# The gated product of two feed-forward blocks, kept in PSUM and split into its halves from there

## The chip, the cores and the metric

The kernel runs on one core of a Trainium2 chip. The metric is the device time of one execution in microseconds (us): a median of several runs of each kernel. The engines are named as the profile names them: PE (TensorE, matmuls), PEld (its weight loads), DVE (VectorE), ACT (ScalarE), POOL (GpSimd) and SP (SyncE, which issues DMAs). SBUF is the working memory of the core; PSUM is the memory into which PE writes, in eight banks.

## The reference

Two layers run over 512 latent tokens and 256 context tokens of width 1024. Layer 0 mixes the tokens with gated DeltaNet and retention heads, layer 1 with differential softmax attention; each layer ends in a gated feed-forward block with 2816 hidden features:

```python
def conv_ffn(h, rows, w_gate, w_up, w_conv, w_down):
    a = h @ w_gate
    a = dwconv2d_centred(a.reshape(bt, rows, lt // rows, D_FF), w_conv).reshape(bt, lt, D_FF)
    return (jax.nn.silu(a) * (h @ w_up)) @ w_down
```

A residual add and a layer norm follow. All inputs are float32. The context tokens pass through the block of layer 0 only, since layer 1 returns latent tokens alone.

## The kernel before

Every large matrix product is made of three: each operand is split into a high half (a copy rounded to fp32r) and a low half (the operand less its high half), and PE sums high by high, high by low and low by high in one PSUM bank. For activations and weights alike the high half is thus a copy on ACT and the low half a subtraction on DVE or POOL. The helper `split` (lines 139 to 148) does this; most weight splits put their low half (`wlo`) on POOL, and their operations all carry lines 147 and 148.

`ffn` (line 1396) is called twice: for layer 0 with 768 tokens (`has_ctx`, "the first block" below, about 690 to 1260 us of the span) and for layer 1 with 512 tokens ("the second block", from about 1685 us to the end). The 2816 hidden features are 22 groups of 128, called f, taken two at a time in 11 steps, called p. For every f, `gate_up` (line 1441) does the following.

- PE makes the gate sum `pg` (tile g_ps) and the up sum `pu` (u_ps) for the 512 latent tokens, each in one bank, and in the first block both for the context in one bank `pc` (c_ps: columns 0 to 255 gate, 256 to 511 up). Each of these tiles has two buffers, so f+2 takes the bank of f.
- ACT (line 1465) writes the middle tap of the 3x3 convolution into the SBUF tile `ac`, and DVE adds the eight others (line 1476), reading g_ps. The context has a convolution of three taps (lines 1480 to 1486).
- ACT takes silu of `ac` in place (line 1487).
- DVE multiplies the up sum by it, back into `ac` (lines 1488, 1490).
- `split` makes the high half `hh` on ACT (line 147) and the low half `hl` on DVE (line 148) from `ac`.

Then (`down`, line 1413, called at line 1522) PE multiplies hh and hl of the step before with a slice of the down weights into d_ps: a group of 6 matmuls for each of the 128-token tiles and each half of the width, 12 groups for a step of the first block and 8 in the second. d_ps has two banks in the first block and four in the second. In the first block DVE takes each group out with a multiplication by the gate (tile gt, line 1425), and line 1523 adds gt to `acc` in SBUF, in turn on POOL and on DVE. In the second block the gate is already in the down weights and DVE adds d_ps straight to `acc` (line 1523). Between steps 0 and 1 DVE multiplies all `acc` tiles by a row of the norm (line 1505: `acc`, `lng` and the result lie in SBUF). After step 10 the last two down products follow, and the layer norm.

Instructions of an engine run in one order. That order is chosen when the program is built, by a planner that goes by priorities (mostly the order of the code) and by its own estimate of when operands will be ready; semaphores are added where an operand or a buffer comes from another engine. So a changed instruction may also take another place among those of its engine.

Of the kernel before, what the change touches and what calls it, by code (L numbers as in the profile page):

```python
# [11 lines left out]
F32 = mybir.dt.float32  # L12
# [11 lines left out]
LAT, CTX = 512, 256  # L24
# [73 lines left out]
class Net:  # L98
# [1297 lines left out]
    def ffn(self, l, has_ctx, acc, dst, key):  # L1396
# [4 lines left out]
        v, g, s_ = nc.vector, nc.gpsimd, nc.scalar  # L1401
# [5 lines left out]
        with ExitStack() as st0:  # L1407
# [5 lines left out]
            def down(w, x, t, n, ps, first=True, last=True, gated=False):  # L1413

                (wh, wl), (xh, xl) = w, x
                steps = [(wi, xi, k) for k in range(2) for xi, wi in ((xh, wh), (xh, wl), (xl, wh))]
                for j, (wi, xi, k) in enumerate(steps):
                    self.mm(ps, xi[:, k, t * P:(t + 1) * P], wi[:, k, n * 512:(n + 1) * 512],
                            start=(first and j == 0), stop=(last and j == len(steps) - 1))
                if not last:  # L1420
                    return
                if gated:
                    return acc[t][:, n * 512:(n + 1) * 512], ps
                gt = gtp.tile([P, 512], F32, tag="gt", name="gt")
                v.tensor_mul(gt, ps, gates[0 if t < NLT else 1][:, n * 512:(n + 1) * 512])  # L1425
                return acc[t][:, n * 512:(n + 1) * 512], gt

            with ExitStack() as st:
                wf = None if key else self.pool(st0, f"wffn{l}", bufs=2)
                fp = self.pool(st, f"ffn{l}", bufs=2)  # L1430
                wf = wf or self.pool(st, f"wffn{l}")
                if key:

                    self.wps = [self.wp]
                else:
                    self.wps = [self.wp, self.wp, wf, wf]
                self.wcount = 0
                gp = self.pool(st, f"ps_g{l}", bufs=2, space=PSUM)
                upp = self.pool(st, f"ps_u{l}", bufs=2, space=PSUM)
                cpp = self.pool(st, f"ps_c{l}", bufs=2, space=PSUM) if has_ctx else None  # L1440
                def gate_up(p):
                    cols = slice(p * 256, (p + 1) * 256)
                    uw = [self.unit([w[:, cols]]) for w in (wg, wu)]
                    hh = hidp.tile([P, 2, NTK], F32R, tag="hh", name="hh")
                    hl = hidp.tile([P, 2, NTK], F32R, tag="hl", name="hl")
                    for i in range(2):
                        f = 2 * p + i
                        cw = [fc[:, t * NFF + f:t * NFF + f + 1] for t in range(9)]
                        pg = gp.tile([P, 512], F32, tag="g", name="g_ps")
                        pu = upp.tile([P, 512], F32, tag="u", name="u_ps")  # L1450
                        pc = cpp.tile([P, 512], F32, tag="c", name="c_ps") if has_ctx else None
                        for j, (w, pl) in enumerate(zip(uw, (pg, pu))):
                            d = [(pl, 0, LAT)]
                            if p == 0:
                                d = [(pl[:, :256], 0, 256), (pl[:, 256:], 256, 256)]
                            if has_ctx:
                                c = (pc[:, j * CTX:(j + 1) * CTX], LAT, CTX)
                                d = [c] + d if p == 0 else d + [c]
                            if p == 0:
                                for one in d:  # L1460
                                    self.proj_fm(w, i * P, [one])
                            else:
                                self.proj_fm(w, i * P, d)
                        ac = fp.tile([P, NTK], F32, tag="ac", name="ac")
                        s_.activation(ac[:, :LAT], pg, AF.Copy, scale=cw[4])  # L1465
                        R, C = LAT // GRID_W, GRID_W
                        av = ac[:, :LAT].rearrange("p (r c) -> p r c", r=R)
                        pv = pg.rearrange("p (r c) -> p r c", r=R)
                        for di in (-1, 0, 1):
                            for dj in (-1, 0, 1):  # L1470
                                if di == 0 and dj == 0:
                                    continue
                                r0, r1 = max(0, -di), R - max(0, di)
                                c0, c1 = max(0, -dj), C - max(0, dj)
                                o = av[:, r0:r1, c0:c1]
                                v.scalar_tensor_tensor(out=o, in0=pv[:, r0 + di:r1 + di, c0 + dj:c1 + dj],  # L1476
                                                       scalar=cw[(di + 1) * 3 + dj + 1], in1=o,
                                                       op0=ALU.mult, op1=ALU.add)
                        if has_ctx:
                            s_.activation(ac[:, LAT:], pc[:, :CTX], AF.Copy, scale=cw[4])  # L1480
                            o = ac[:, LAT + 1:TOK]
                            v.scalar_tensor_tensor(out=o, in0=pc[:, 0:CTX - 1], scalar=cw[3], in1=o,
                                                   op0=ALU.mult, op1=ALU.add)
                            o = ac[:, LAT:TOK - 1]
                            v.scalar_tensor_tensor(out=o, in0=pc[:, 1:CTX], scalar=cw[5], in1=o,
                                                   op0=ALU.mult, op1=ALU.add)
                        s_.activation(ac, ac, AF.Silu)  # L1487
                        v.tensor_mul(ac[:, :LAT], pu, ac[:, :LAT])  # L1488
                        if has_ctx:
                            v.tensor_mul(ac[:, LAT:], pc[:, CTX:], ac[:, LAT:])  # L1490
                        self.split(ac, hh[:, i, :], hl[:, i, :], v)
                    hid[p] = (hh, hl)

                self.lo_engs, self.lo_count = "v" if l else "vgvv", 0
                gate_up(0)
                if key:
                    self.wps = [wf, self.wp, self.wp, self.nextw]
                    self.wcount = 0
                lnb = self.row(self.pool(st, f"flnb{l}"), a["ln_b"][l, 0], "lnb")
                rst = ExitStack()  # L1500
                lng = self.row(self.pool(rst, f"flng{l}"), a["ln_g"][l, 0], "lng")
                for r in (lng, lnb):
                    self.pin(s_.activation(r, r, AF.Copy, scale=ALPHA))
                for t in tiles:
                    self.pin(v.tensor_mul(acc[t], acc[t], lng))  # L1505
                gate_up(1)
                self.lo_engs = "g"
                self.cparts = 1
                gates = self.gate_rows(lnp, l, 1, 2 if has_ctx else 1)
                last = None if key else self.affine_rows(lnp, l, 1)  # L1510
                rst.close()
                gtp = self.pool(st, f"fgt{l}", bufs=GTB)
                for p in range(1, NP):
                    if p > 1:
                        gate_up(p)
                    if p < NP - 1:
                        w = self.unit_rows(wd[(p - 1) * 256:p * 256, :], None if key else gates[0])
                        x = hid.pop(p - 1)
                        for t in tiles:
                            for n in range(2):  # L1520
                                ps = dp.tile([P, 512], F32, tag="d", name="d_ps")
                                o, gt = down(w, x, t, n, ps, gated=not key)
                                (v if n or not key else g).tensor_add(o, o, gt)
                    if 2 <= p < 2 + len(tiles):
                        t = tiles[p - 2]
                        self.pin(g.tensor_add(acc[t], acc[t], lnb))
                if key:
                    self.wps = [self.wp]
                ws = [self.unit_rows(wd[p * 256:(p + 1) * 256, :], None if key else gates[0]) for p in (NP - 2, NP - 1)]
# [5 lines left out]
            with ExitStack() as st:  # L1535
# [6 lines left out]
                for gi, grp in enumerate(groups):  # L1542
# [6 lines left out]
                    for t in grp:  # L1549
                        st_ = self.ln_stats()  # L1550
                        for n in range(2):
                            if gi == 0:
                                ps = pss[t, n]
                            else:
                                ps = next(dps).tile([P, 512], F32, tag="d", name="d_ps")
# [290 lines left out]
```

## Time and profile before

| what | value |
|---|---|
| median of 3 runs | 2064.56 us (2062.54 to 2068.04) |
| profiled execution, own time | 2061.71 us |
| its span, first to last instruction | 2059.9 us |
| mean granted PE clock | 0.98 of full |
| busy: PE, PEld, DVE, ACT, POOL | 94%, 81%, 60%, 35%, 38% |

The profile is of one execution, taken by the hardware profiler; durations below are from it. "Busy" counts the time in which an engine executes. A timeline row gives the start and the length of one instruction, or of several merged ones (x2), and in brackets how long the engine had been idle before it, and which instruction ended that wait. In the lists by line, three durations stand for the shortest, the median and the longest.

### The profile page before, as it was taken

How to read it: one execution, taken by the hardware profiler on the slowest of the kernel's cores; microseconds unless marked ns; L12 is line 12 of the kernel's file. 1: busy time of each engine (PE TensorE's matmuls, PEld its weight loads, DVE VectorE, ACT ScalarE, POOL GpSimd, SP SyncE). 2: the span in 40 equal slices, each digit the busy share in tenths (PEclk: the TensorE clock that was granted, in tenths of full speed). 3: DMA queues.
4: the chain of work that ended last, by engine and by line, in shares of the span. 5: the costliest groups of instructions: out<-in, count | busy, mean ns of one | idle time of the engine just before them, and what ended most of it. 6: DMA issues, size and time to landing. Idle time of an engine off the chain costs nothing. (4 is left out here: it accounts for less than half of the span.)

```text
span 2059.9 us, 33511 instructions
## 1 busy us (share of the span) xinstructions
PE 1940.8 (94%) x13766; PEld 1669.9 (81%) x13766; DVE 1229.4 (60%) x2430; ACT 721.5 (35%) x1273; POOL 776.3 (38%) x416
## 2 busy tenths in 40 slices
PE   7999999999898999999999998999997989999997
PEld 5877677788898988888888887989886987888886
DVE  3344645443467686666666656456667687756667
ACT  4432343433334522222222225454555343323221
POOL 1233223212322254554544434122213126756572
PEclk9999999999999999999999999999998999999999
DMA  9456334465624221111111112011103143323221
GB/s 290 129 169 181 111 116 141 133 179 175 184 74 132 93 82 62 62 62 62 62 62 62 62 62 90 21 42 42 42 32 103 52 144 102 99 85 102 82 82 41
DMA packets 198113, 201.33 MB, mean 98 GB/s; under 512 B 21336, under 2 KB 186808, under 8 KB 197960
## 3 DMA queue, kind: packets, MB, share of 16 engines
q1 hardware_dynamic: 195832, 196.78, 30.4%
q10 hardware_dynamic: 2128, 2.41, 0.4%
q8 instruction: 108, 1.77, 0.4%
q14 instruction: 45, 0.37, 0.1%
HBM read 185.89 MB, written 13.27 MB: 97 GB/s over the span
## 5 line engine op out<-in xcount | busy, mean ns | idle before, releaser
L148 POOL TENSOR_TENSOR wlo<-raw,whi 128x512 fp32r<-128x512 f32 (+2 forms) x158 | 416.5, 2657 | 498.4 <-ACT whi L147 457.3
L1476 DVE SCALAR_TENSOR_TENSOR ac<-g_ps,fconvT,ac 128x441 f32<-128x441 f32 (+2 forms) x352 | 243.9, 694 | 190.9 <-ACT ac L1465 181.2
L147 ACT CAST whi<-raw 128x2048 fp32r<-128x2048 f32 (+2 forms) x183 | 201.3, 1136 | 382.5 <-PE d_ps L115 162.5
L115 PE MATMUL d_ps<-whi,hh 128*128 128x512 f32 x440 | 175.8, 400 | 11.2 <-DVE gt L1425 6.6
L115 PE MATMUL d_ps<-whi,hl 128*128 128x512 f32 x440 | 173.2, 394 | 0.6 <-DVE hl L148 0.6
L115 PE MATMUL d_ps<-wlo,hh 128*128 128x512 f32 x440 | 173.0, 393 | 0.0
L115 PE MATMUL opj<-whi,hTh 128*128 128x256 f32 x512 | 147.5, 288 | 2.1 <-ACT oq L1628 1.6
L115 PE MATMUL g_ps<-hTl,whi 128*128 128x512 f32 (+1 forms) x384 | 145.1, 378 | 3.2 <-POOL hTl L148 3.2
L115 PE MATMUL opj<-whi,hTl 128*128 128x256 f32 x512 | 146.0, 285 | 0.0
L115 PE MATMUL opj<-wlo,hTh 128*128 128x256 f32 x512 | 145.0, 283 | 0.0
L115 PE MATMUL u_ps<-hTh,whi 128*128 128x512 f32 (+1 forms) x384 | 144.6, 377 | 0.0
L115 PE MATMUL u_ps<-hTh,wlo 128*128 128x512 f32 (+1 forms) x384 | 144.6, 377 | 0.0
L115 PE MATMUL g_ps<-hTh,whi 128*128 128x512 f32 (+1 forms) x384 | 144.6, 377 | 0.0
L115 PE MATMUL u_ps<-hTl,whi 128*128 128x512 f32 (+1 forms) x384 | 144.5, 376 | 0.0
L115 PE MATMUL g_ps<-hTh,wlo 128*128 128x512 f32 (+1 forms) x384 | 144.3, 376 | 0.0
L115 PE MATMUL fpj<-whi,hTh 128*128 128x256 f32 x432 | 125.6, 291 | 1.1 <-ACT fo L717 1.1
L115 PE MATMUL fpj<-wlo,hTh 128*128 128x256 f32 x432 | 125.1, 290 | 0.0
L115 PE MATMUL fpj<-whi,hTl 128*128 128x256 f32 x432 | 124.1, 287 | 0.0
L115 PEld LDWEIGHTS d_ps<-whi,hh 128*128 128x128 f32 x440 | 83.0, 189 | 38.4 <-DVE gt L1425 16.9
L115 PEld LDWEIGHTS opj<-whi,hTh 128*128 128x128 f32 x512 | 97.7, 191 | 4.2 <-ACT oq L1628 2.6
L115 PE MATMUL c_ps<-hTh,wlo 128*128 128x256 f32 x352 | 98.9, 281 | 0.0
L115 PE MATMUL c_ps<-hTh,whi 128*128 128x256 f32 x352 | 98.8, 281 | 0.0
(459 smaller groups left out, 4999.1 us busy)
## 6 DMA issues: line engine op xcount, KB each, us to landing
mraw<-in_mod_w_dram SPq DMA_DIRECT2D x80, 512.0 KB
raw<-in_f_w_gate_dram SPq DMA_DIRECT2D x22, 1024.0 KB
raw<-in_f_w_up_dram SPq DMA_DIRECT2D x22, 1024.0 KB
raw<-in_f_w_down_dram SPq DMA_DIRECT2D x22, 1024.0 KB
raw<-in_o_w_qkv_dram SPq DMA_DIRECT2D x12, 1024.0 KB
raw<-in_e_w_in_dram SPq DMA_DIRECT2D x9, 1024.0 KB
mraw<-in_mod_w_dram SPq DMA_DIRECT2D x32, 256.0 KB
raw<-in_e_w_in_dram SPq DMA_DIRECT2D x8, 512.0 KB
```

What stands on the lines that cost most here:

```text
L115: self.nc.tensor.matmul(out, lhsT=lhsT, rhs=rhs, start=start, stop=stop)
L147: self.nc.scalar.copy(h, r)
L148: lo_eng.tensor_sub(l, r, h.bitcast(F32))
L1476: v.scalar_tensor_tensor(out=o, in0=pv[:, r0 + di:r1 + di, c0 + dj:c1 + dj], scalar=cw[(di + 1) * 3 + dj + 1], in1=o, op0=ALU.mult, op1=AL ...
```

## The change

The product of silu and the up sum is written back into the bank of the up sum instead of into `ac`. Its high half is copied by ACT from that bank, and its low half is formed by DVE from the bank and the high half. In the first block this is done separately for the 512 latent and the 256 context tokens, so that there are two copies and two subtractions for each f where there was one of each; the multiplications were two already. In the second block the number of instructions stays. The results go to the same tiles `hh` and `hl`. The bank of the up sum now stays in use until the subtraction; `ac` is free after the multiplication.

```diff
                         s_.activation(ac, ac, AF.Silu)
-                        v.tensor_mul(ac[:, :LAT], pu, ac[:, :LAT])
-                        if has_ctx:
-                            v.tensor_mul(ac[:, LAT:], pc[:, CTX:], ac[:, LAT:])
-                        self.split(ac, hh[:, i, :], hl[:, i, :], v)
+
+                        for t0, n, ps in ((0, LAT, pu),) + (((LAT, CTX, pc[:, CTX:]),) if has_ctx else ()):
+                            v.tensor_mul(ps, ps, ac[:, t0:t0 + n])
+                            s_.copy(hh[:, i, t0:t0 + n], ps)
+                            v.tensor_sub(hl[:, i, t0:t0 + n], ps, hh[:, i, t0:t0 + n].bitcast(F32))
```

## Rows read from the trace of the kernel before

**Rows 1.** The page, busy time: us, share of the span, number of instructions.
```profile
PE 1940.8 (94%) x13766; PEld 1669.9 (81%) x13766; DVE 1229.4 (60%) x2430; ACT 721.5 (35%) x1273; POOL 776.3 (38%) x416
```

**Rows 2.** Waits of PE, whole span: who waited for whom, us, times, longest.
```profile
PE d_ps L115 <- DVE gt L1425: 6.6, 18, 0.6
...
PE d_ps L115 <- DVE acc L1523: 4.3, 1, 4.3
...
PE d_ps L115 <- DVE hl L148: 0.6, 1, 0.6
```

**Rows 3.** Timeline of DVE, second block, step 1: start us, length us.
```profile
1721.94 4.04 DVE L148 TENSOR_TENSOR hl<-ac,hh 128x512 fp32r<-128x512 f32 x1
1725.91 2.94 DVE L1476 SCALAR_TENSOR_TENSOR ac<-g_ps,fconvT,ac 128x448 f32<-128x448 f32 x4
1728.76 0.68 DVE L1523 TENSOR_TENSOR acc<-acc,d_ps 128x512 f32<-128x512 f32 x1
```

**Rows 4.** Timeline of POOL at the same place.
```profile
1720.82 4.61 POOL L148 TENSOR_TENSOR wlo<-raw,whi 128x2048 fp32r<-128x2048 f32 x1
```

**Rows 5.** Timeline of PE at the same place.
```profile
1729.49 0.50 PE L115 MATMUL d_ps<-whi,hh 128*128 128x512 f32 x1 [4.28 <-DVE acc L1523]
...
1736.69 0.40 PE L115 MATMUL g_ps<-hTh,whi 128*128 128x512 f32 x1
```

**Rows 6.** Busy time by stretch: PE, PEld, DVE, ACT, POOL; then granted clock.
```profile
797.00:815.00 18.00, 17.19 (x80) 13.54 (x79) 15.46 (x21) 4.13 (x7) 12.98 (x9) 1.00 0.38 117
...
1730.30:1734.00 3.70, 3.70 (x11) 2.88 (x10) 3.54 (x7) 0.75 (x2) 0.50 (x1) 0.54 0.53 142
```

**Rows 7.** Multiplications of acc, second block: ns shortest, median, longest.
```profile
L1505 DVE TENSOR_TENSOR acc<-acc,lng x4: 1212/1214/5041, 1707.1 to 1714.3; 128x1024 f32<-128x1024 f32 x4
```

**Rows 8.** The products with the up sum on DVE: ns shortest, median, longest.
```profile
L1488 DVE TENSOR_TENSOR ac<-u_ps,ac x44: 680/692/693, 702.5 to 2027.4; 128x512 f32<-128x512 f32 x44
```

**Rows 9.** The low halves hl of the second block, same columns.
```profile
L148 DVE TENSOR_TENSOR hl<-ac,hh x22: 692/1121/4041, 1699.9 to 2028.8; 128x512 fp32r<-128x512 f32 x22
```

**Rows 10.** Groups by form on DVE and ACT: busy us, mean ns, idle before.
```profile
L1108 DVE TENSOR_TENSOR hTl<-yT_ps,hTh 128x512 fp32r<-128x512 f32 x8 | 5.5, 689 | 1.2 <-ACT hTh L1107 1.1
...
L1108 DVE TENSOR_TENSOR hTl<-yT_ps,hTh 128x256 fp32r<-128x256 f32 x8 | 3.3, 414 | 0.6 <-ACT hTh L1107 0.6
...
L1700 ACT ACTIVATE sc<-sc,mx 128x768 f32<-128x768 f32 x32 | 28.0, 875 | 18.1 <-DVE mx L1697 17.4 <-DVE oss L1727 0.5
...
L147 ACT CAST hh<-ac 128x768 fp32r<-128x768 f32 x22 | 18.4, 836 | 27.5 <-DVE ac L1490 27.5
...
L1739 ACT CAST hTh<-yT_ps 128x512 fp32r<-128x512 f32 x8 | 4.6, 583 | 11.3 <-PE yT_ps L119 11.3
```

**Rows 11.** Timeline of DVE, first block, one down product (step 2).
```profile
806.00 1.67 DVE L1523 TENSOR_TENSOR acc<-acc,gt 128x512 f32<-128x512 f32 x1
807.60 0.68 DVE L1425 TENSOR_TENSOR gt<-d_ps,gate 128x512 f32<-128x512 f32 x1
808.20 1.43 DVE L148 TENSOR_TENSOR hl<-ac,hh 128x768 fp32r<-128x768 f32 x1
809.55 0.68 DVE L1425 TENSOR_TENSOR gt<-d_ps,gate 128x512 f32<-128x512 f32 x1
810.26 1.05 DVE L1523 TENSOR_TENSOR acc<-acc,gt 128x512 f32<-128x512 f32 x1
811.24 1.43 DVE L1425 TENSOR_TENSOR gt<-d_ps,gate 128x512 f32<-128x512 f32 x2
```

**Rows 12.** Timeline of POOL at the same place.
```profile
807.08 3.68 POOL L1523 TENSOR_TENSOR acc<-acc,gt 128x512 f32<-128x512 f32 x2
```

**Rows 13.** Timeline of PE at the same place.
```profile
808.33 0.50 PE L115 MATMUL d_ps<-whi,hh 128*128 128x512 f32 x1 [0.59 <-DVE gt L1425]
...
811.97 0.50 PE L115 MATMUL d_ps<-whi,hh 128*128 128x512 f32 x1
```

**Rows 14.** Timeline of DVE, first block, the last low half (step 10).
```profile
1219.92 2.82 DVE L148 TENSOR_TENSOR hl<-ac,hh 128x768 fp32r<-128x768 f32 x1 [0.96 <-ACT hh L147]
```

## The prediction

> **What bounds the kernel now.** I read the page's busy times first: PE is busy for 94% of the span [rows 1], so only an edit that shortens PE's waits, or its matmuls, can shorten the kernel. DVE, which does most of the edited work, has 40% of its time free; what it does while PE does not wait for it counts for nothing. So the second view is the list of PE's waits. In the two feed-forward blocks three of them are for DVE's work around the edit [rows 2]: once for 4.3 us, for line 1523 to empty a bank of d_ps; 18 times, 6.6 us in all, for line 1425 to do so; and once 0.6 us for a low half hl. The third view is the timeline of DVE ahead of each of these waits, to see whether the edited instructions stand in the queue there. They do in all three.
>
> The third thing to see is why they are long. The same subtraction hl<-ac,hh takes 692 ns at its shortest and 4041 at its longest [rows 9]. The longest starts at 1721.94 and ends at 1725.98 [rows 3]; POOL has one instruction from 1720.82 to 1725.43 [rows 4]. So the subtraction ends 0.55 us after POOL does, about its own length less its start-up: it stood still until POOL was through. The four multiplications of line 1505 say the same: one took 5041 ns, the shortest 1212 [rows 7]. All these read two operands from SBUF. The product of line 1488 reads one from PSUM and one from SBUF, and its 44 durations lie between 680 and 693 ns [rows 8], though POOL is busy 38% of the time [rows 1]. An instruction with one PSUM operand is not held up by POOL. The change gives the low half exactly that form.
>
> **The change part by part.**
>
> *The subtraction.* The nearest rows are those of line 1108, a low half from PSUM: 689 ns for 512 columns, 414 for 256 [rows 10]. I take these. In the second block one of 689 replaces one of 692 to 4041; in the first block two, 0.69 + 0.41 = 1.10 us, replace one that took 1.43 to 2.82 in the places that matter [rows 11, 14].
>
> [...]
>
> *The product, now written into PSUM.* No row of before shows DVE writing PSUM. Below, it could be a little cheaper than line 1488; ACT reads and writes one bank in 875 ns for 768 columns, against 836 for a copy of 768 in SBUF [rows 10], a gain or a loss of a few hundredths. Above, the worst that I can price is a bank that serves reading and writing in turn, which doubles 0.69 and 0.41. I take the same price as now, since the nearest rows lie within 5%, and keep the double for a rival.
>
> *The copy on ACT.* 583 ns from PSUM for 512 columns (line 1739) against 836 from SBUF for 768 [rows 10]; with a second copy of some 0.4 us the first block pays about 0.15 us more per f, on an engine that is 35% busy. The latent copy no longer waits for the context's product, so the chain to the first subtraction gets shorter. I count nothing; uncovered it would be 0.15 us at the one place where PE waits for hl itself.
>
> *The banks held longer.* The up sum's bank is freed after product, copy and subtraction, 0.69 + 0.58 + 0.69, some 1.4 us later than now. In the second block the low half of the third f ends at 1725.98, and PE needs that bank only in step 2, which begins at 1736.69 [rows 3, 5]. No wait; cost nothing. No DMA is issued, added or passed by any moved step.
>
> *A: the 4.3 us wait (second block, step 1).* DVE runs hl 4.04, then four taps 2.94, then the first line 1523, at whose end PE goes on (1728.76 + 0.68 = 1729.44; PE at 1729.49) [rows 3, 5]. With hl at 0.69 all this is 4.04 - 0.69 = 3.35 us earlier: PE goes on at 1726.14, after 0.9 us instead of 4.28. [...] Across a down product of the first block, with its wait of 0.6 us, it stays 1.00 [rows 6], so I take it that a wait of 0.9 leaves it there: 3.70 x (1 - 0.54) = 1.70 us more. A = 3.35 + 1.70 = 5.05 us. What is late next is nothing: the three later line 1523s stand one tap apart on DVE, 0.68 + 0.67, and PE needs a bank every 1.4 us. Should the clock fall all the same, A is 3.35.
>
> *B: the waits for line 1425 (first block).* The 18 waits are two in each of nine down products. In the one shown, DVE is busy without a gap from 806.00 to 812.7, and PE follows it: its groups start at 808.33 and 811.97, as line 1425 frees a bank (its second merged row: the first of two ends near 811.93) [rows 11, 13]. Here hl occupies 808.20 to 809.55, 1.35 us. Two subtractions take 0.69 + 0.41 less the 0.08 by which neighbours overlap in these rows (807.60 + 0.68 against 808.20), twice: 0.94. So at least 0.41 us. Then the addition at 810.26 takes 1.05 although 0.69 is the usual length of 512 columns: it ends 0.55 after POOL's two additions (807.08 + 3.68 = 810.76) [rows 12], so it is held by them, and hl, with two SBUF operands, stands in POOL's way just before. Free of hl, POOL may end earlier, and the addition would lose some of its 0.36 of stall besides: 0.6 or somewhat more in all. I take 0.5, nearer to what the rows show: B = 9 x 0.5 = 4.5 us, with 3.7 and, at 0.6, 5.4 as ends.
>
> *C: the last low half of the first block.* It took 2.82 us [rows 14]; the latent and context subtractions take 1.10 and are done 1.7 us earlier, before PE comes for them. C = 0.6 us, the wait [rows 2].
>
> Elsewhere the product chain is beside PE's work and moves nothing. Sum: 5.05 + 4.5 + 0.6 = 10.2 us. The profiled execution's own 2061.71 us (span 2059.9) would become 2051.5; it lies 2.85 below the median of the runs shown, 2064.56, and against that median the forecast is 2054.4.
>
> **The rivals.**
>
> 1. *Another order in the first block.* The latent subtraction is ready earlier than hl was; the planner may set it ahead of the line 1425 at 807.60. Then PE's group waits 0.6 us longer at 808.33 and only some 0.2 us per product are won: B = 1.8, total 7.5, 2057.1. For it: gate_up stands ahead of the down product in the code. Against: in that place the addition comes first in any case.
> 2. *A is not won.* The planner puts more taps, or the subtraction itself, ahead of line 1523, or the next operation with two SBUF operands is held by the same POOL instruction. Then only B + C = 5.1 remain: 2059.5. For it: four taps already stand between. Against: they read PSUM and aren't held.
> 3. *It does not do what it says*: the subtractions from PSUM are held by POOL all the same. Nothing moves but two more instructions per f: 2064.6. Against: the 44 rows of line 1488.
> 4. *Slower: the product into its own bank is dear.* Its place is B, where both products stand in DVE's gapless queue. If DVE reads and writes one bank in turn, each down product gains 0.5 and loses 1.1: B = -5.4, A = 5.05 - 0.69 = 4.4, C = 0.6, sum about 0. From that point on, the double price, it is slower: at three times, B = 9 x (0.5 - 2.2) = -15.3, A = 3.7, together -11 us: 2075. Against: ACT's rows in PSUM. For: nothing shows DVE doing it.
>
> **How the numbers follow.** Forecast 0.52; rival 1 0.14; rival 2 0.14; rival 3 0.08; rival 4, and whatever reordering costs as much, 0.12. Runs of this kernel differ by up to 0.3% from one another, and 0.3% (6.2 us) is about what a measurement can tell from no change. Faster by more: all but little of the forecast and most of rival 1, 0.62; slower by more: rival 4, 0.12; between: 0.26. The likeliest time is 2054.4. The forecast's own range comes from A between 3.4 and 5.9 (POOL's earlier instructions are no longer held by hl either), B between 3.7 and 5.4: 2052 to 2057. The range for 8 of 10 takes in rivals 1 to 3: 2050 to 2064.8.
>
> **What would show it.** Right: no hl above 0.70 us (512) or 0.42 (256) in the changed trace, PE's wait for line 1523 at 1 us or below with a granted clock of 1.0 behind it, PE's waits for line 1425 about half of 6.6 us, none for hl. Rival 1: an L148-like subtraction ahead of the third line 1425. Rival 4: products well above 0.69 us. Wrong altogether: PE waiting for u_ps or c_ps, or a new wait of several us in step 1 of either block.

## The result, and the profile after

The changed kernel takes 2049.99 us, median of 12 runs (2043.47 to 2060.38), beside 2062.36 for the kernel before in 12 runs of its own (2057.59 to 2068.15): ratio 0.9945, 95% interval 0.9929 to 0.9961 (estimated from all these runs; the two medians alone give 0.9940). The forecast, 2054.4 against 2064.56, is a ratio of 0.9951. As an absolute time the result lies at the lower end of the range, 0.01 us under 2050: before's own median was 2.2 us lower in these runs than the 2064.56 from which the forecast started, and the medians lie 12.4 us apart instead of 10.2. The profiled execution of after took 2056.78 us (span 2055.0), one of the longer ones of the 12.

Single executions of one kernel differ by 10 us and more, and the traces show where most of that arises: the first gate matmul of the first feed-forward block, ahead of which no edit here changes the order of any engine, starts between 679.0 and 689.6 us in the twelve profiles of this study. So I compare stretches, which begin at matmuls of PE: *block 1* from its first gate matmul (679.0 us in before) to the first out-projection matmul behind it, *block 2* from its first gate matmul (1669.1 us in before) to the end of the span. Profiled a second time, after gave block 1 569.7 instead of 569.3, and block 2 385.1 again.

| us | block 1 | between | block 2 |
|---|---|---|---|
| before | 576.7 | 413.3 | 390.8 |
| after | 569.3 | 413.8 | 385.1 |
| difference | -7.4 | +0.5 | -5.7 |
| forecast | -5.1 (B + C) | 0 | -5.05 (A) |

Both stretches became shorter by more than forecast. The page of after, its busy times (it answers to [rows 1]):

```profile
PE 1940.2 (94%) x13766; PEld 1674.1 (81%) x13766; DVE 1199.5 (58%) x2452; ACT 721.6 (35%) x1295; POOL 765.1 (37%) x416
```

PE's work is the same. DVE has 22 instructions more and is busy 29.9 us less; POOL, whose instructions are untouched, is busy 11.2 us less. The waits of PE in after (answering to [rows 2]; who waited for whom, us in total, times, longest):

```profile
PE d_ps L115 <- DVE gt L1425: 4.4, 9, 0.5
...
PE d_ps L115 <- ACT hh L1491: 0.6, 1, 0.6
```

The 4.3 us wait for the addition (line 1524 now) has no line here any more. Of the 18 waits for line 1425, 9 are left. The 0.6 us wait for hl is now one for hh.

**Second block, step 1.** DVE in after, to be laid beside [rows 3] (start us, length us):

```profile
1721.92 0.69 DVE L1492 TENSOR_TENSOR hl<-u_ps,hh 128x512 fp32r<-128x512 f32 x1
1722.53 2.94 DVE L1476 SCALAR_TENSOR_TENSOR ac<-g_ps,fconvT,ac 128x448 f32<-128x448 f32 x4
1725.38 0.68 DVE L1524 TENSOR_TENSOR acc<-acc,d_ps 128x512 f32<-128x512 f32 x1
```

POOL and PE at the same place (beside [rows 4, 5]), and the stretch with the granted clock near its end (beside [rows 6]):

```profile
1720.91 4.65 POOL L148 TENSOR_TENSOR wlo<-raw,whi 128x2048 fp32r<-128x2048 f32 x1
```
```profile
1725.63 0.39 PE L115 MATMUL d_ps<-whi,hl 128*128 128x512 f32 x1
1726.12 0.50 PE L115 MATMUL d_ps<-whi,hh 128*128 128x512 f32 x1
```
```profile
1730.30:1734.00 3.70, 3.70 (x18) 3.02 (x17) 3.24 (x6) 2.50 (x2) 0.33 (x2) 1.00 0.66 181
```

The subtraction starts within 0.03 us of where it started before, POOL is in the midst of the same kind of instruction as then, and the subtraction takes 0.69 instead of 4.04. The four taps and the addition follow in the same order; the addition starts at 1725.38, which is 3.38 earlier. From the start of the last matmul ahead of PE's wait for it to the start of the first behind it are 0.49 us; before it was 4.66 (1724.83 to 1729.49). The earlier of these two matmuls of before:

```profile
1724.83 0.39 PE L115 MATMUL d_ps<-whi,hl 128*128 128x512 f32 x1
```

The granted clock stays at 1.00 over these 3.70 us, where 0.54 had been granted.

**First block, step 2.** DVE, POOL and PE in after, to be laid beside [rows 11 to 13]:

```profile
812.80 1.67 DVE L1524 TENSOR_TENSOR acc<-acc,gt 128x512 f32<-128x512 f32 x1
814.40 0.68 DVE L1492 TENSOR_TENSOR hl<-u_ps,hh 128x512 fp32r<-128x512 f32 x1
815.00 0.41 DVE L1492 TENSOR_TENSOR hl<-c_ps,hh 128x256 fp32r<-128x256 f32 x1
815.33 1.27 DVE L1425 TENSOR_TENSOR gt<-d_ps,gate 128x512 f32<-128x512 f32 x2
816.63 1.28 DVE L1524 TENSOR_TENSOR acc<-acc,gt 128x512 f32<-128x512 f32 x1
```
```profile
808.86 5.07 POOL L148 TENSOR_TENSOR wlo<-raw,whi 128x512 fp32r<-128x512 f32 x4 [2.55 <-ACT whi L147]
813.87 1.76 POOL L1524 TENSOR_TENSOR acc<-acc,gt 128x512 f32<-128x512 f32 x1
```
```profile
815.20 0.40 PE L115 MATMUL g_ps<-hTl,whi 128*128 128x512 f32 x1
816.06 0.50 PE L115 MATMUL d_ps<-whi,hh 128*128 128x512 f32 x1 [0.46 <-DVE gt L1425]
816.40 0.40 PE L115 MATMUL d_ps<-wlo,hh 128*128 128x512 f32 x1
```

Two things differ from the order of before: both subtractions stand ahead of the third line 1425, and PE has nine matmuls of the next step (g_ps and c_ps, up to 815.20) ahead of the waiting down matmul, where it had three. It waits once in the step. Before it went like this (PE of before, the rows between those of [rows 13]):

```profile
807.35 0.40 PE L115 MATMUL g_ps<-hTl,whi 128*128 128x512 f32 x1
...
808.66 0.40 PE L115 MATMUL d_ps<-wlo,hh 128*128 128x512 f32 x1
...
809.81 0.28 PE L115 MATMUL c_ps<-hTl,whi 128*128 128x256 f32 x1
810.28 0.50 PE L115 MATMUL d_ps<-whi,hh 128*128 128x512 f32 x1 [0.19 <-DVE gt L1425]
810.61 0.39 PE L115 MATMUL d_ps<-wlo,hh 128*128 128x512 f32 x1
...
811.54 0.40 PE L115 MATMUL d_ps<-whi,hl 128*128 128x512 f32 x1
...
812.31 0.40 PE L115 MATMUL d_ps<-wlo,hh 128*128 128x512 f32 x1
```

What a wait costs is read from the starts here. Undisturbed, the next matmul starts 0.235 us after one of 512 columns and 0.12 after one of 256; and the start behind a wait's first matmul comes after 0.34 instead of 0.235. In before, the gaps to 808.33, 810.28 and 811.97 are 0.98, 0.47 and 0.43 long, so 0.745, 0.35 and 0.195 too long; with the slow starts behind them, 0.095, 0.095 and 0.105, the step loses 1.59 us. In after the gap to 816.06 is 0.86, 0.625 too long, and with 0.105 behind it the step loses 0.73. The difference, 0.86 us per step, is the whole gain of a step: over steps 2 to 10 the first context tap (line 1482) of a step's second f follows that of the step before after 51.63 us in before ((1215.40 - 802.39) / 8) and after 50.77 in after ((1215.38 - 809.19) / 8).

**The last low half.** PE, DVE and ACT at the end of the first block (before: [rows 14]):

```profile
1219.56 0.50 PE L115 MATMUL d_ps<-whi,hh 128*128 128x512 f32 x1 [0.58 <-ACT hh L1491]
```
```profile
1218.52 0.42 DVE L1490 TENSOR_TENSOR c_ps<-c_ps,ac 128x256 f32<-128x256 f32 x1
1219.27 0.69 DVE L1492 TENSOR_TENSOR hl<-u_ps,hh 128x512 fp32r<-128x512 f32 x1 [0.32 <-ACT hh L1491]
```
```profile
1219.13 0.38 ACT L1491 CAST hh<-c_ps 128x256 fp32r<-128x256 f32 x1
```

The subtraction takes 0.69 instead of 2.82, and PE waits as long as before, for the copy on ACT ahead of it: PE comes 3 us earlier, after 18 matmuls of the last products instead of 32. From the last line 1482 to the end of block 1 it is 40.7 us, before 40.4.

**The edited operations,** all of after (ns shortest, median, longest; beside [rows 8 to 10]):

```profile
L1490 DVE TENSOR_TENSOR u_ps<-u_ps,ac x44: 689/699/700, 710.3 to 2022.5; 128x512 f32<-128x512 f32 x44
L1490 DVE TENSOR_TENSOR c_ps<-c_ps,ac x22: 422/423/423, 710.9 to 1218.5; 128x256 f32<-128x256 f32 x22
```
```profile
L1492 DVE TENSOR_TENSOR hl<-u_ps,hh x44: 676/692/694, 711.6 to 2023.8; 128x512 fp32r<-128x512 f32 x44
L1492 DVE TENSOR_TENSOR hl<-c_ps,hh x22: 406/414/415, 712.2 to 1219.9; 128x256 fp32r<-128x256 f32 x22
```

No subtraction is held anywhere, and the product written into its own bank costs 7 ns more than the one into SBUF. Laid beside POOL's rows, all low halves of the two traces say the same. In before, 24 of the 44 start while an instruction of POOL is in flight. They take 1.0 to 4.04 us, and each ends 0.55 us (512 columns) or 0.82 us (768) behind the end of that instruction, however long it is; the other 20 take 0.69 and 0.96. In after, 35 of the 66 start so, and none of them takes over 0.69 us (512) or 0.42 (256), like the other 31.

### The profile page after: what moved, and what is told of

The parts are those of the page before. It is cut to its first block, busy times and chain, and to the rows that moved or that the text cites. A ratio compares the mean times of both kernels' runs of the same rounds, so it can differ in the third digit from the quotient of the medians.

```text
span 2055.0 us, 33529 instructions
## 1 busy us (share of the span) xinstructions
PE 1940.2 (94%) x13766; PEld 1674.1 (81%) x13766; DVE 1199.5 (58%) x2452; ACT 721.6 (35%) x1295; POOL 765.1 (37%) x416
## 3 DMA queue, kind: packets, MB, share of 16 engines
q8 instruction: 108, 1.77, 0.4%
## 5 line engine op out<-in xcount | busy, mean ns | idle before, releaser
L1425 DVE TENSOR_TENSOR gt<-d_ps,gate 128x512 f32<-128x512 f32 x120 | 81.7, 686 | 29.7 <-PE d_ps L115 28.8
```

## The experiments

Ten runs follow: eight new kernels, after once more (e8) and one of the eight once more (e10). Each ratio is to runs of the kernel before made beside it.

**e1 and e2: each block alone.** The diff is against after: the new lines in one block, the old ones in the other.

```
+ if not has_ctx:
      for t0, n, ps in ((0, LAT, pu),) + (((LAT, CTX, pc[:, CTX:]),) if has_ctx else ()):
...
+ else:
+     v.tensor_mul(ac[:, :LAT], pu, ac[:, :LAT])
+     if has_ctx:
+         v.tensor_mul(ac[:, LAT:], pc[:, CTX:], ac[:, LAT:])
+     self.split(ac, hh[:, i, :], hl[:, i, :], v)
```

This is e1; e2 has `if has_ctx:`.

> Only the second block (layer 1) is changed, the first is as before. Stretches read from the trace: first block, from its first gate matmul to the first matmul of the next layer's projection (before 576.8 us, changed kernel 569.3); second block, from its first gate matmul to the end (before 390.8, changed 385.1). Theory (the low half, with one PSUM operand, is no longer held by POOL, PE's one long wait goes, and the clock behind it stays up): second block 385.1, first block 576.8, whole time 5.7 us below before, ratio 0.997. Rival (the gain is one of order or of something in the first block that carries over): second block above 388, ratio 0.999 or more.

> Only the first block (layer 0) is changed, the second is as before. Theory: first block 569.3 us, second block 390.8 with its wait of 4.3 us for line 1523 still there; whole time 7.5 us below before, ratio 0.996. Rival (the two edits act on one another, through the planner's order or the weights' arrival): the second block differs from 390.8 by more than 1 us.

e1: 2055.89 us (2050.74 to 2062.94), ratio 0.9977 [0.9961, 0.9992]; block 1 576.7, block 2 385.0. e2: 2055.33 (2048.11 to 2062.67), ratio 0.9969 [0.9951, 0.9987]; block 1 569.9, block 2 391.1. Each block has after's length where it is changed and before's where it is not, to 0.6 us, and the two ratios multiplied give 0.9946, where after's is 0.9945: the gains add up. PE's waits in e2 show each in its place (and e1's the other way round):

```profile
PE d_ps L115 <- DVE acc L1529: 4.5, 1, 4.5
PE d_ps L115 <- DVE gt L1425: 4.5, 9, 0.5
```

**e3: the form of the change without its point.** Two parts, in the same order of engines, but the product goes to SBUF and the halves are taken from there:

```
- v.tensor_mul(ps, ps, ac[:, t0:t0 + n])
- s_.copy(hh[...], ps)
- v.tensor_sub(hl[...], ps, hh[...])
+ at = ac[:, t0:t0 + n]
+ v.tensor_mul(at, ps, at)
+ s_.copy(hh[...], at)
+ v.tensor_sub(hl[...], at, hh[...])
```

> The product goes to SBUF as before, but copy and subtraction are done in two parts, latent and context, as in the changed kernel; PE's order in the first block is then the changed kernel's up to its last step. This separates the new order from the PSUM operand. Theory (holding by POOL is what counts): the subtractions in SBUF are held again, each down product loses what it won, first block 574 to 577 us; second block as before, 390.8, one subtraction of 4 us; whole time 0 to 3 us below before. Rival (the new order, in which PE fills its wait with matmuls of the next step, is what counts in the first block): first block 569 to 571, whole time 6 to 8 us below before.

2064.46 us (2059.22 to 2071.03), ratio 1.0014 [0.9997, 1.0031]; block 1 579.0, block 2 391.8. DVE and PE in step 2, and PE's waits of the whole:

```profile
807.93 1.67 DVE L1524 TENSOR_TENSOR acc<-acc,gt 128x512 f32<-128x512 f32 x1
809.53 2.12 DVE L1492 TENSOR_TENSOR hl<-ac,hh 128x512 fp32r<-128x512 f32 x2
811.57 1.28 DVE L1425 TENSOR_TENSOR gt<-d_ps,gate 128x512 f32<-128x512 f32 x2
```
```profile
812.30 0.50 PE L115 MATMUL d_ps<-whi,hh 128*128 128x512 f32 x1 [1.59 <-DVE gt L1425]
```
```profile
PE d_ps L115 <- DVE gt L1425: 14.4, 9, 1.6
```

The two subtractions take 2.12 us instead of the 1.01 of after, and PE, whose order is that of after, waits 1.59 instead of 0.46. So the parts and the new order alone are worth nothing: block 1 is 2.3 us longer than before. That is 2 us above the longest that I expected, since one wait of 1.59 in place of two short ones was not in my sum. The PSUM operand is worth 579.0 - 569.3 = 9.7 us in this order.

**e4: the other party made short.** The kernel before, with the splits of the second block's gate and up weights, ACT's copies and POOL's low halves, cut into four:

```
- self.cparts = 1
+ self.cparts = 1 if has_ctx else 4
```

> The kernel before, but in the second block, from step 2 on, ACT and POOL split the gate and up weights in four pieces of 512 columns instead of one of 2048, so that POOL's instructions are 1.3 us long instead of 4.6; PE's order is the same. Theory (a VectorE instruction with two SBUF operands stands still until POOL's instruction in flight has ended): no low half over 2.0 us (4.04 before), the wait of PE for line 1523 falls by 2 us or more, second block 386 to 388.5. Rival (the long subtractions are slow for another reason, as the memory's load by DMA or ACT): a low half of 3 us or more remains, second block 390 or more.

2059.68 us (2051.35 to 2066.82), ratio 0.9989 [0.9974, 1.0005]: as a total not to be told from no change. Block 2, though, is 386.0, and the subtraction that had taken 4.04:

```profile
1722.36 0.76 DVE L148 TENSOR_TENSOR hl<-ac,hh 128x512 fp32r<-128x512 f32 x1
```
```profile
PE d_ps L115 <- DVE acc L1523: 1.0, 1, 1.0
```

It reads SBUF twice as before. POOL's instruction of 4.61 us is no longer beside it; there are two, of 2.42 and 2.85 us, and the subtraction starts 0.2 us before the first of them ends:

```profile
1720.15 5.23 POOL L197 TENSOR_TENSOR raw<-raw,gate 128x1024 f32<-128x1024 f32 x2 [4.94 <-DMA raw<-in_f_w_down_dram]
```

PE waits 1.0 us, and block 2 is 4.8 us shorter without the change. So the 4.3 us came from one long instruction of POOL. One part of the expectation failed: a low half of 2.12 us is left in a later step of the block, where none above 2.0 was expected. Two caveats: what stands here is the scaling of weights, not one of the cut pieces, which come later; and three taps, not four, follow the subtraction, 0.72 us that shorter instructions did not bring.

**e5: the same cure for the addition.** What is left per step, 0.73 us, stands behind an addition that is still held (1.67 in after, step 2). In the first block the gated product of the second column half now stays in its bank, so that the addition reads one operand from PSUM:

```
- gt = gtp.tile([P, 512], F32, tag="gt", name="gt")
+ gt = ps if n else gtp.tile([P, 512], F32, tag="gt", name="gt")
```

> As after, but in the first block the gated down product of the second column half stays in its d_ps bank, so that VectorE's addition of line 1524 has one PSUM operand as the subtraction now has. Theory (what is left of the first block's loss, 0.46 us of TensorE waiting for line 1425 in each of nine steps, is the addition of line 1524 held by GpSimd: 1.67 and 1.28 us against 0.69 unheld): the addition takes 0.68 to 0.70 everywhere, the waits for gt of line 1425 (4.4 us in nine) fall under 1 us, and the first block's stretch goes from 569.3 to 563.5-566.5 us, the whole to about 2045-2047. Rival (a bank is now held 0.69 us longer, through the addition, and there are only two): TensorE waits for acc of line 1524 instead, once or several times a step, and the first block's stretch is 570 us or more. The second block's stretch stays at 385 by both.

2043.31 us (2037.99 to 2051.32), ratio 0.9907 [0.9883, 0.9931]; block 1 566.5. Line 1524 in e5 and in after, and PE's busy time over 440 us of the first block in e5 and in after (us of the stretch, then PE busy):

```profile
L1524 DVE TENSOR_TENSOR acc<-acc,d_ps x126: 675/686/690, 754.4 to 1984.2; 128x512 f32<-128x512 f32 x126
```
```profile
L1524 DVE TENSOR_TENSOR acc<-acc,gt x54: 691/693/2970, 762.1 to 1183.6; 128x512 f32<-128x512 f32 x54
```
```profile
739.10:1179.10 440.00, 440.00 (x2303) 374.51 (x2302) 256.37 (x406) 102.53 (x146) 212.46 (x117) 1.00 0.19 63
```
```profile
746.70:1186.70 440.00, 435.60 (x2280) 370.83 (x2279) 271.39 (x405) 101.89 (x145) 216.95 (x116) 1.00 0.19 63
```

No addition is held, none of the nine waits is left, PE is busy without a gap: the theory, against the rival of the bank held longer. A step takes 50.27 us ((1203.42 - 801.24) / 8), 0.50 less than in after. But block 1 became only 2.8 to 3.2 us shorter, not the 4.5 that nine such steps make, and lies at the upper end of what was expected: from the last line 1482 to its end it is 42.2 us, where after's two profiles have 40.7 and 40.6. Something was given back in the last group.

**e6: the order that the prediction had assumed.** The subtractions of the first block planned later:

```
- v.tensor_sub(hl[...], ps, hh[...])
+ with self.priority(200 if has_ctx else 0): v.tensor_sub(hl[...], ps, hh[...])
```

> As after, but in the first block both subtractions are planned behind the third and fourth products of line 1425 instead of ahead of them (the place that the prediction gave them); TensorE's order differs only in that it runs three matmuls of the next step, not nine, ahead of the waiting down matmul. Theory A (the subtractions ahead of line 1425 are what TensorE waits for, 0.46 us a step): the wait goes and the first block's stretch falls from 569.3 to 565-566.5. Theory B (the wait is the addition of line 1524 held by GpSimd, which the order of the work does not allow for; six matmuls less to run, 6 x 0.175 = 1.05 us, take back what the 1.02 us of subtractions moved give): the waits for gt of line 1425 stay at 0.4-0.6 us a step and the first block's stretch at 568-570.5.

2053.97 us (2050.84 to 2056.77), ratio 0.9955 [0.9938, 0.9973]; block 1 572.2, 2.5 to 2.9 longer than after's two. PE in step 2, and its waits:

```profile
811.96 0.40 PE L115 MATMUL g_ps<-hTl,whi 128*128 128x512 f32 x1
812.98 0.50 PE L115 MATMUL d_ps<-whi,hh 128*128 128x512 f32 x1 [0.63 <-DVE gt L1425]
...
815.61 0.39 PE L115 MATMUL d_ps<-whi,hl 128*128 128x512 f32 x1
815.92 0.50 PE L115 MATMUL d_ps<-whi,hh 128*128 128x512 f32 x1
```
```profile
PE d_ps L115 <- DVE gt L1425: 5.4, 9, 0.6
```

Theory A is out: with the subtractions behind line 1425 PE waits no less. Theory B has the mechanism, but 572.2 is above its 570.5: I left out that the later subtraction pushes the fifth product of line 1425, so that a second wait opens at 815.92, too short for a bracket. By starts the step loses 0.785 + 0.105 + 0.075 + 0.105 = 1.07 us, 0.34 more than in after; the steps are 51.14 us apart, 0.37 more.

**e7 and e10: e5 with the subtractions 40 places later,** and the same again:

> As e5_add_from_psum, with the first block's subtractions planned 40 places later (one of them behind the third product of line 1425). If the held addition is the whole of what is left, this gives nothing beyond e5_add_from_psum: first block within 1 us of it. If the place of the subtractions is part of it, it is 1 to 4 us below e5_add_from_psum in the first block.

> e7_both once more, beside e9 on the same chip: 2041-2044 us, first block 565.6 +- 0.5, no wait of TensorE for line 1425.

e7: 2041.63 us (2040.61 to 2043.71), ratio 0.9897 [0.9877, 0.9917]; e10: 2042.12 (2037.73 to 2047.94), ratio 0.9914 [0.9887, 0.9941]; block 1 565.6 in both. That is 0.9 below e5, just within the 1 us that I had called nothing: once no addition is held, the place of the subtractions hardly counts. Block 1 is 3.7 us below after's here; how the whole times compare is said under e8.

**e8: after again,** beside e5 to e7:

> The changed kernel itself, on the same chip as the three others, so that they can be compared with it directly: 2047-2056 us, first block's stretch 569.3 +- 1, second block's 385.1 +- 0.5.

2049.4 us (2047.27 to 2055.72), ratio 0.994 [0.992, 0.9961]; 569.7 and 385.1. Its interval and e7's don't overlap, so e7 takes less time than after; e10's, against other runs of before, reaches over its lower end by 0.002.

**e9: the gated product in PSUM in the loop alone.**

```
- gt = ps if n else gtp.tile([P, 512], F32, tag="gt", name="gt")
+ gt = ps if n and first else gtp.tile([P, 512], F32, tag="gt", name="gt")
```

> As e7_both, but the gated product stays in its PSUM bank in the loop's nine down products alone; in the last group (line 1559, from which the layer norm goes on) it goes to SBUF as in after. In e5 and e7 the stretch from the last line 1482 of the first block to the first out-projection matmul took 42.3 and 42.2 us, against 40.6 and 40.7 in two profiles of after. If the order that the PSUM form brought to the last group is what cost this 1.6 us, the stretch is 40.7 +- 0.4 again, the first block 564 us and the whole 1 to 2 us below e7_both; if it comes from the last steps arriving with nothing left to wait for (the loss only moved down), it stays at 42 and the first block at 565.6.

The stretch from the last line 1482 is 40.6 us, block 1 563.9: both as expected, if the order of the last group was the cause. In that stretch PE is idle for 4.85 us in e7 and for 3.39 in e9 and in e8, and three waits make the difference. These are their rows in e7, and the first two in e9, where the third wait is absent:

```profile
1234.96 0.41 PE L119 MATMUL ln_ps<-ident,acc 128*128 128x128 f32 x2 [0.70 <-issue]
1240.81 0.41 PE L119 MATMUL ln_ps<-ident,acc 128*128 128x128 f32 x2 [1.55 <-ACT acc L1274]
...
1246.81 0.44 PE L119 MATMUL ln_ps<-ident,acc 128*128 128x128 f32 x2 [0.69 <-DVE hf L1314]
```
```profile
1241.99 0.41 PE L119 MATMUL ln_ps<-ident,acc 128*128 128x128 f32 x2 [0.23 <-issue]
1247.52 0.41 PE L119 MATMUL ln_ps<-ident,acc 128*128 128x128 f32 x2 [1.23 <-ACT acc L1274]
```

The total was not lower: 2047.07 (2037.47 to 2051.46), ratio 0.9931 [0.9906, 0.9957]. From the first gate matmul of block 1 to the end, e9's profile has 1360.0 us, e7's 1360.0 and e10's 1361.2 (before 1380.9, after 1368.2 and 1366.1). The 1.7 us that block 1 gained are made up for by a longer stretch between the blocks (411.0 against 409.2) when e9 is laid beside e7, and in part beside e10 (410.4); that this is more than the spread of this stretch is not shown. The profiled execution of e9 is longer than theirs by what lies ahead of its first gate matmul, which comes at 689.6. e9 and e7 can't be ranked by these runs.

## Why the prediction was right, and where it was not

**What holds whom: right.** In before, the subtractions of DVE with two SBUF operands that started while POOL worked stood until its instruction was through (24 of 24); with a PSUM operand they didn't: in after, 66 subtractions no more than 2 ns above their median; in e3, with the same parts in SBUF, 66 between 410 and 4824 ns; in e5, 54 additions of at most 690 ns that had taken up to 2970. For 512 columns beside an instruction of POOL it was at most 694 ns from PSUM in after, up to 4041 ns with two SBUF operands in before.

**A: right.** The prediction has the addition 3.35 us earlier; it is 3.38. The granted clock stayed at 1.00 as assumed, where before had 0.54 over the same 3.70 us [rows 6]. Block 2 gained 5.7 instead of 5.05. The surplus is the 0.8 us by which DVE is ahead relative to the block's start when it comes to this place: it reaches the product at 1720.57 in after and 1720.56 in before, though block 2 starts at 1669.9 instead of 1669.1. So the gap in PE's matmuls is 4.17 us shorter (0.49 for 4.66), and about 1.6 are left for the clock, where 1.70 were forecast. The lead comes from POOL: two of its splits ahead of this place, which ran beside a low half, took 1.75 to 1.77 and 5.07 us in before, e2 and e3, and 1.29 to 1.33 and 4.62 to 4.65 in the eight profiles with the second block changed. The prediction had named that in its range (5.9: "POOL's earlier instructions are no longer held by hl either"). Rival 2 is out.

**B: right in kind, mis-sized, and by another way than described.** It was priced at 0.5 us per step and is 0.86. Two things were wrong. The order: the prediction left the subtractions between the two products of line 1425, as in [rows 11]. The planner chose rival 1's order, and its sign, a subtraction ahead of the third line 1425, is in the trace; but rival 1's price (0.2 per step) fails as well, since it left PE where it was; the planner also set six more matmuls ahead of PE's wait and made one wait of three. And the size of a wait: the prediction saw two waits and took idle time. The two with a bracket stand at 808.33 and 810.28; that at 811.97, which it took for the second, is a third, without a bracket. The two bracketed ones cost some 0.25 us more than their brackets say (0.84 for [0.59]), so that by these starts fewer waits are cheaper than more; no run tests that alone. e6 has nearly the order assumed: block 1 is 4.5 us below before there, and a step loses 0.52 us less than in before. That is B as forecast, C being 0 there too.

**C: failed.** The prediction's "done 1.7 us earlier, before PE comes for them" held PE's arrival fixed. It moved 3 us earlier with the rest of the order, and the wait of 0.6 became one of 0.58 for the copy. C is 0. The prediction had counted nothing for the copy, "uncovered it would be 0.15 us at the one place where PE waits for hl itself": the place was right, but it is now the whole wait there. This was read from the trace, not tested.

**The sum: near, in part by luck.** By the profiles the two blocks gained 13.1 us where 10.2 were forecast: A missed by +0.7, B by +3.2 (9 x 0.86 = 7.7 for 4.5), C by -0.6. The ratio of the whole, 0.9945, is 11.3 us of before's 2062.36 and so nearer to the forecast than the blocks are. The stretches outside them, which the prediction took as unchanged, vary by some us from profile to profile, so that part of this nearness is chance.

**The rest.** Rivals 3 and 4 are out by the durations above: nothing held, and writing PSUM in place costs 699 against 692. The ACT row that the prediction set against rival 4 (line 1700, 768 columns) is not of one bank: its tile has 1024 columns of fp32, twice those of g_ps or u_ps, which are one bank each. So it said less about working in place in a bank than was made of it. The subtraction from PSUM was no dearer than the one from SBUF: 692 ns for 512 columns and 414 for 256 (medians in after), where an unheld one of 512 columns from SBUF took 692 to 694 in before.

## What to carry to other kernels

Where DVE's time for one form varies from its usual length to several times that, see which engine ends just ahead of it; giving the operation a PSUM operand that is there anyway freed it here for 7 ns a product, and the engine on the other side too. The new order that comes with it can cost something elsewhere (1.6 us in the last group of e5 and e7). Count what a wait costs from the starts of the matmuls around it, not from its bracket, and count the short ones. A gain on a planned kernel comes with a new order of all engines: the forecast should say what it is worth with the waiting engine's order as it is and with it moved.

## What the runs showed of the hardware

- An fp32 subtraction of DVE with two SBUF operands that started while an instruction of POOL was in flight ended 0.55 us (512 columns) or 0.82 us (768) behind that instruction's end, 24 times of 24 in before.
- The hold worked both ways: POOL's instructions are untouched, and its busy time fell from 776.3 us in before to 765.1 in after, where DVE's subtractions no longer read SBUF twice.
- DVE multiplied a PSUM bank in place by an SBUF operand, 512 columns of fp32, in 699 ns (44 times in after, 689 to 700), and 256 in 423.
- A matmul of 512 columns behind a wait took 0.50 us in the records instead of 0.40, and the next one started 0.33 to 0.34 us after it instead of 0.235, at a granted clock of 1.00 (step 2 of before and after).
